# Dense attention's score matmuls: 289 contraction rows cut into two passes of 128 and a shared pass of 33, instead of 97, 96 and 96

## The chip, the cores and the metric

The kernel runs on one core of one Trainium2 chip. The metric is device time in microseconds of one execution. Of the core's engines, TensorE (PE) multiplies, with a separate path for its weight loads (PEld), VectorE is DVE, ScalarE is ACT, GpSimd is POOL, and SyncE (SP) issues most DMAs.

## The reference

One layer of a transformer over 1024 latent tokens and 256 context tokens. The part that the change touches is group B of its attention, eight heads of latent attention, dense over all 1280 keys:

```python
def mla_attend(qn, qr, kn, kr, v):
    s = (jnp.einsum('bqhd,bkhd->bhqk', qn, kn, preferred_element_type=jnp.float32)
         + jnp.einsum('bqhr,bkr->bhqk', qr, kr, preferred_element_type=jnp.float32)) * MLA_SCALE
    p = jax.nn.softmax(s, axis=-1)
    o = jnp.einsum('bhqk,bkhd->bqhd', p.astype(v.dtype), v)
    return o.reshape(qn.shape[0], qn.shape[1], H_B * V_B)
```

`qn` and `kn` have 64 values per head, `qr` and `kr` have 32 (`kr` is shared by the heads). Before it stand the input projection and a windowed attention (group A), after it the output projection, a router, and 16 experts.

## The kernel before, in words

All matmuls that matter are in fp32r. Where one factor alone isn't exact enough, a value is split into a high part and the remainder (`split`), and a product is taken as high x high + high x low + low x high. For a score that is 3 x 96 rows of contraction, and one row more that adds the negative maximum of the query's scores, so that the exponential needs no bias: 289 rows. The kernel before holds them in four tiles per head: `kh` (97 rows: 64 of `kn`, 32 of `kr`, one of ones) and `kl` (96 rows, the low parts) for the keys, `qh` (97 rows, the last one the negative maximum) and `ql` for the queries.

Dense attention (group B) is a loop over 160 units, 8 heads x 2 halves of the queries x 10 blocks of 128 keys (`Runner.run`, which emits the program in order). A unit's scores are a tile of 128 keys by 512 queries in a PSUM bank "s", from three matmuls (`s_b`, L1093 to L1095). ACT takes the exponential twice, into `ph` (rounded, L614) and again in full (L615), in place for the even units and into the buffer `pf` for the odd ones. The difference, `pl`, is made by DVE for even units and by POOL for odd ones (L1098). Four units later, three matmuls add the unit to the head's output in a bank "x" (`pv_b`, L1107 to L1109).

Between the units stand the steps that prepare the next head (`prep_b`, spread over the 20 units of the head before): `kprep` splits its keys (L954 to L960), `tr` transposes its queries (L976) and splits them (L978, L979), `mxp` and `mxq` multiply queries and keys once more for the maxima (L983, L990, in banks "m", reduced by DVE at L985 and L992), and `fin2` sends the negative maxima as a row to `qh` (L1005, a DMA that POOL issues). Head 0 is prepared before the loop, mixed with the rest of the key and value projection (`kn_mm`, L875, evacuated by ACT at L877). `kr_copy` (L932) copies the rows of `kr`, which are the same for all heads, to the second pair of key tiles.

Other work hangs in the same loop: `mod_rest` streams 8 MB of modulation weights through the staging tiles (`stage`), and `load_wo` loads the output projection's weights, 1 MB a call, into them. After the loop `omm` (L1138) multiplies the first 128 tokens of the mixed heads with these weights, split by `wo_split` one after the other. The last 128 rows of the mix, from the last two heads, come back from memory at L1205 (`mix7`).

Elsewhere in the program, matmuls use few rows of the array at L564 (one row, `finish_fast`) and L1540 (two rows, `pick2` of the experts). The built program gives every matmul the part of the array, the tile, that it uses: these two have 32 of its 128 rows, L1108 has all rows and 64 columns, the router's L1353 and the matmuls named above have the whole array.

Of the kernel before, what the change touches and what calls it, by code (L numbers as in the profile page):

```python
# [10 lines left out]
F32 = mybir.dt.float32  # L11
F32R = mybir.dt.float32r
# [5 lines left out]
PSUM = bass.MemoryType.PSUM  # L18
DRAM = bass.MemoryType.DRAM

D = 1024
S = 1024
# [3 lines left out]
NK = NT + NCT  # L26
# [12 lines left out]
def f32(ap):  # L39
    return ap.bitcast(F32)  # L40
# [7 lines left out]
def tile_backbone(ctx: ExitStack, tc, x, c, ctxt, c_ctx, w_mod, b_mod, norm_attn, norm_ffn, w_in,  # L48
# [104 lines left out]

    psa = Pool("psa", space=PSUM)

    def bank(tag, shape=(128, 512)):
        return psa.tile(list(shape), F32, tag, bufs={"s": 3, "x": 2, "m": 3}[tag])

    qaf = qa.rearrange("p t e -> p (t e)")
    brow, mr = qaf[0:1, 0:2 * D], qaf[0:4, 2 * D:4 * D]  # L160
# [764 lines left out]
    kn, vb = B2["kn"], B2["vb"]  # L925

    pbk2 = Pool("pbk2")
    khs = [pbk2.tile([97, NK * 128], F32R, f"kh{i}") for i in range(2)]
    kls = [pbk2.tile([96, NK * 128], F32R, f"kl{i}") for i in range(2)]
    pbq = Pool("pbq")  # L930

    def kr_copy():  # L932
        act.copy(khs[1][64:96, :], f32(khs[0][64:96, :]))
        act.copy(kls[1][64:96, :], f32(kls[0][64:96, :]))

    for (t0, t1), pt in zip(TG, krt):
        sl = slice(t0 * 128, t1 * 128)
        split(act, dve, khs[0][64:96, sl], kls[0][64:96, sl], pt[:32, :(t1 - t0) * 128])
    for q in range(2):
        dve.tensor_copy(khs[q][96:97, :], ones[0:1, 0:1].to_broadcast([1, NK * 128]))  # L940
# [4 lines left out]

    def prep_b(h):
        st = {}
        kh, kl, vv = khs[h % 2], kls[h % 2], vh[h % 2]
        steps = []

        def kprep():
            src = kn[:, h // 2]
            if h % 2 == 0:
                act.activation(kh[0:64, :], src[0:64], AF.Copy)  # L954
                pool.tensor_sub(kl[0:64, :], src[0:64], f32(kh[0:64, :]))
            else:
                scr = pbq.tile([128, NK * 128], F32R, "scr")
                act.activation(kh[0:64, :], src[64:128], AF.Copy)
                dve.tensor_copy(scr[64:128], src[64:128])
                pool.tensor_sub(kl[0:64, :], src[64:128], f32(scr[64:128]))  # L960

        def vprep():
            src = vb[:, :, h * 64:(h + 1) * 64]
            dve.tensor_copy(vv[:, :, 0:64], src)
            pool.tensor_sub(vv[:, :, 66:130], src, f32(vv[:, :, 0:64]))

        def alloc():
            st["q"] = pbq.tile([97, S], F32R, "qh", bufs=2)
            st["l"] = pbq.tile([96, S], F32R, "ql", bufs=2)
            QB[h] = (st["q"], st["l"], kh, kl, vv)  # L970
            st["m"] = pbq.tile([128, 8, 3], F32, "mx", bufs=2)

        def tr(b):
            pt = bank("m")
            for j in range(4):
                pe.transpose(pt[:96, j * 128:(j + 1) * 128], qb[:, 4 * b + j, h * 96:(h + 1) * 96], ident)  # L976
            sl = slice(b * 512, (b + 1) * 512)
            act.activation(st["q"][0:96, sl], pt[:96], AF.Copy)  # L978
            dve.tensor_sub(st["l"][:, sl], pt[:96], f32(st["q"][0:96, sl]))  # L979

        def mxp(t, j):
            pm = bank("m")
            pe.matmul(pm, st["q"][0:96, t * 128:(t + 1) * 128], kh[0:96, j * 512:(j + 1) * 512],  # L983
                      start=True, stop=True)
            dve.tensor_reduce(out=st["m"][:, t, j:j + 1], in_=pm, axis=AX.X, op=OP.max)  # L985

        def mxq(t):
            pm = bank("m").rearrange("p (a b) -> p a b", a=2)
            for j in range(2):
                pe.matmul(pm[:, j], st["q"][0:96, (t + j) * 128:(t + j + 1) * 128], kh[0:96, 1024:1280],  # L990
                          start=True, stop=True)
            dve.tensor_reduce(out=st["m"][:, t:t + 2, 2], in_=pm, axis=AX.X, op=OP.max)  # L992

        def fin():
            nm = pbq.tile([128, 8], F32, "nm", bufs=2)
            dve.tensor_reduce(out=nm, in_=st["m"], axis=AX.X, op=OP.max, negate=True)
            st["nm"] = nm

        def fin2():
            nm = st["nm"]  # L1000
            pt = bank("m")
            pe.transpose(pt[:8, :128], nm, ident)
            rr = pbq.tile([8, 128], F32R, "rr", bufs=2)
# [42 lines left out]

    wof = {}
    NX = 6
    slots = [0, 1, 2, 3]

    def stage():
        n = slots.pop(0)
        slots.append(n)
        return (wms if n < 4 else wms2 if n < 6 else wms3 if n < 6 + NX else pm).tile([128, 2, D], F32, f"wst{n}")

    def load_wo(k):
        w = stage()
# [26 lines left out]
    R.add(150, lambda: early_mix(0, 3))  # L1084
    R.add(151, lambda: early_mix(3, 7))

    def s_b(u, un):
        h, hf, kc, first, last = un
        qh, ql, kh, kl, vv = QB[h]
        ps = bank("s")  # L1090
        ks = slice(kc * 128, (kc + 1) * 128)
        qs = slice(hf * 512, (hf + 1) * 512)
        pe.matmul(ps, kh[:, ks], qh[:, qs], start=True, stop=False)  # L1093
        pe.matmul(ps, kh[0:96, ks], ql[:, qs], start=False, stop=False)  # L1094
        pe.matmul(ps, kl[:, ks], qh[0:96, qs], start=False, stop=True)  # L1095
        on_dve = not (u % 2 and u < len(units) - 8)
        pf, ph, lo = softmax_parts(pbt, ps, SC_B, on_dve)
        return ph, lo, lambda: (dve if on_dve else pool).tensor_sub(lo, pf, f32(ph))  # L1098

    def pv_b(u, un, pp):  # L1100
        h, hf, kc, first, last = un
        ph, lo, _ = pp
        vv = QB[h][4]
        if first:
            xo[h, hf] = bank("x", (65, 512))
        xx = xo[h, hf]
# [14 lines left out]
                    R.add(R.u + d, f)  # L1121

    late_b = R.run(units, s_b, pv_b, 4)
    psa.close()
# [689 lines left out]
```

## Time and profile before

| what | us |
|---|---|
| median of 3 runs | 1218.68 (1218.54 to 1219.02) |
| the profiled execution's time | 1217.52 |
| its span, first to last instruction | 1215.8 |
| dense attention's units in the span | 440.3 to 719.8 |

Busy time over the whole span: PE 92%, PEld 69%, DVE 73%, ACT 58%, POOL 38%. TensorE's granted clock is 0.959 of full speed on average. These shares are means over stages with different limits, so the stage that is changed has to be read by itself. In rows of the trace the first number is the start in microseconds from the span's start, the second the duration; a matmul's record is longer than the time that it keeps the array from the next one.

### The profile page before, as it was taken

To read this page: it belongs to the slowest core of one execution; us is meant where nothing else is said; L and a number is where in the kernel's file an instruction comes from. 1 tells how busy PE (TensorE), PEld (TensorE's weight loads), DVE (VectorE), ACT (ScalarE), POOL (GpSimd) and SP (SyncE) were. 2 spreads that over 40 slices of the span, in tenths; PEclk is the share of its full clock that TensorE was granted. 3 is DMA by queue.
4 is the path that set the end of the run, shared out by engine and by line. 5 is a ranking of instruction groups with operands and counts; after the bars stand their busy time and mean duration, and the time that the engine had idled before them with its cause. 6 is when DMAs were issued, how large, how long until landed. Compare 5 with 4: busy or idle time off the path is not lost. (4 is left out here: it accounts for less than half of the span.)

```text
span 1215.8 us, 15361 instructions
## 1 busy us (share of the span) xinstructions
PE 1115.5 (92%) x5168; PEld 838.1 (69%) x5168; DVE 884.1 (73%) x1511; ACT 700.6 (58%) x1122; POOL 463.7 (38%) x453
## 2 busy tenths in 40 slices
PE   7799998899999889999999999996499999999993
PEld 1687886576667567776666577885377887778872
DVE  5767764656874466777777256588789999999986
ACT  5623223567776447776676772223176776777753
POOL 0042322455443244665655432442314243332214
PEclk9899999999999889999999999997599999999996
DMA  7714320001211110212010525755799999999727
GB/s 297 298 59 131 129 76 1 1 15 23 66 28 23 22 73 32 88 53 87 17 45 10 187 74 200 243 194 206 277 319 371 375 371 386 370 397 372 279 51 278
DMA packets 68622, 198.27 MB, mean 163 GB/s; under 512 B 15894, under 2 KB 24243, under 8 KB 63423
## 3 DMA queue, kind: packets, MB, share of 16 engines
q1 hardware_dynamic: 60224, 178.73, 40.5%
q0 software_dynamic: 5152, 18.52, 5.7%
q8 instruction: 40, 0.66, 0.2%
q10 hardware_dynamic: 3168, 0.06, 0.1%
q14 instruction: 38, 0.31, 0.1%
HBM read 172.34 MB, written 24.78 MB: 162 GB/s over the span
## 5 line engine op out<-in xcount | busy, mean ns | idle before, releaser
L1409 DVE TENSOR_TENSOR wl<-wst,wh 128x2048 fp32r<-128x2048 f32 x95 | 215.9, 2287 | 22.3 <-ACT wh L1403 22.3
L1403 ACT ACTIVATE wh<-wst 128x2048 fp32r<-128x2048 f32 x96 | 183.8, 1917 | 71.8 <-PE u L1580 39.3
L614 ACT ACTIVATE ph<-s 128x512 fp32r<-128x512 f32 x236 | 140.8, 597 | 92.5 <-PE s L1095 75.9
L1098 POOL TENSOR_TENSOR pl<-pf,ph 128x512 fp32r<-128x512 f32 x76 | 102.2, 1355 | 68.2 <-ACT pf L615 46.1
L1098 DVE TENSOR_TENSOR pl<-s,ph 128x512 fp32r<-128x512 f32 x84 | 57.0, 680 | 54.6 <-ACT s L615 54.6
L985 DVE TENSOR_REDUCE mx<-m 128x1 f32<-128x512 f32 x128 | 83.1, 682 | 14.3 <-PE m L983 14.1
L615 ACT ACTIVATE s<-s 128x512 f32<-128x512 f32 x123 | 73.1, 594 | 0.0
L1093 PE MATMUL s<-qh,kh 97*128 97x512 f32 x160 | 66.1, 413 | 5.2 <-DVE pl L1098 2.7
L1626 PE MATMUL y<-wh,shf 128*128 128x512 f32 x240 | 69.4, 400 | 0.0
L615 ACT ACTIVATE pf<-s 128x512 f32<-128x512 f32 x113 | 66.9, 592 | 0.0
L772 POOL TENSOR_TENSOR pl<-pf,ph 128x512 fp32r<-128x512 f32 x37 | 47.7, 1289 | 49.2 <-ACT pf L615 45.9
L122 POOL TENSOR_SCALAR rstd<-ss 128x1 f32<-128x1 f32 x36 | 12.9, 358 | 134.6 <-ACT sjunk L193 64.6
L1094 PE MATMUL s<-ql,kh 96*128 96x512 f32 x160 | 64.1, 401 | 0.0
L1107 PE MATMUL x<-ph,vh 128*65 128x512 f32 x160 | 63.8, 399 | 0.0
L1095 PE MATMUL s<-qh,kl 96*128 96x512 f32 x160 | 63.6, 397 | 0.0
L1108 PE MATMUL x<-ph,vh 128*64 128x512 f32 x160 | 63.3, 396 | 0.0
L1109 PE MATMUL x<-pl,vh 128*65 128x512 f32 x160 | 63.2, 395 | 0.0
L329 PE MATMUL s<-wih,hb 128*128 128x512 f32 (+2 forms) x224 | 57.7, 381 | 3.3 <-ACT hb L81 3.3
L1548 POOL DMA_INDIRECT xg<-h2d,ix x16 | 23.6, 1473 | 91.4 <-PE t L1564 36.4
L1643 POOL DMA_INDIRECT accd<-yt,ix x7 | 34.7, 4959 | 61.2 <-DVE yt L1636 61.2
L81 ACT ACTIVATE hb<-xt 128x512 fp32r<-128x512 f32 (+1 forms) x22 | 13.0, 593 | 69.2 <-DVE xt L245 69.1
L1643 POOL DMA_INDIRECT accd<-gab,ix x8 | 25.3, 3164 | 70.1 <-DVE gab L1636 70.1
(491 smaller groups left out, 3135.9 us busy)
## 6 DMA issues: line engine op xcount, KB each, us to landing
wst<-in_w_gate_dram SPq DMA_DIRECT2D x63, 512.0 KB
wst<-in_w_up_dram SPq DMA_DIRECT2D x63, 512.0 KB
wst<-in_w_down_dram SPq DMA_DIRECT2D x31, 1024.0 KB
mw<-in_w_mod_dram SPq DMA_DIRECT2D x32, 256.0 KB
wst<-in_w_mod_dram SPq DMA_DIRECT2D x8, 1024.0 KB
wi<-in_w_in_dram SPq DMA_DIRECT2D x8, 720.0 KB
wi<-in_w_mod_dram SPq DMA_DIRECT2D x9, 512.0 KB
h2d<-h SPq DMA_DIRECT2D x8, 520.0 KB
```

Source lines behind the costliest of these rows:

```text
L614: act.activation(ph, ps, AF.Exp, scale=scale)
L615: act.activation(pf, ps, AF.Exp, scale=scale)
L985: dve.tensor_reduce(out=st["m"][:, t, j:j + 1], in_=pm, axis=AX.X, op=OP.max)
L1093: pe.matmul(ps, kh[:, ks], qh[:, qs], start=True, stop=False)
L1094: pe.matmul(ps, kh[0:96, ks], ql[:, qs], start=False, stop=False)
L1095: pe.matmul(ps, kl[:, ks], qh[0:96, qs], start=False, stop=True)
L1098: return ph, lo, lambda: (dve if on_dve else pool).tensor_sub(lo, pf, f32(ph))
L1107: pe.matmul(xx, vv[:, kc, 0:65], ph, start=first, stop=False)
L1108: pe.matmul(xx[0:64], vv[:, kc, 66:130], ph, start=False, stop=False)
L1403: act.activation(W[i][0], staged[i], AF.Copy)
L1409: eng.tensor_sub(lo, staged.pop(i), f32(hi))
L1626: pe.matmul(py[n], a[:, k], w[b][:, n], start=(k == 0 and m == 0), stop=(k == 3 and m == 2))
```

## The change

The 289 rows are laid out anew. A first pass of 128 rows has `kn` and `kr` high with `qn` and `qr` high, and 32 rows of `kn` low with `qn` high. A second has `kn` and `kr` high with `qn` and `qr` low, and the other 32 rows of `kn` low with `qn` high. The rest is 33 rows: `kr` low with `qr` high, and the row of ones with the negative maximum. That rest is held twice, in `k3` and `q3` on partitions 0 to 32 and 64 to 96. For every two units (two blocks of keys) two matmuls of 33 rows are issued first, one from each half of the partitions, into two banks; then each unit follows with its two passes of 128 rows. The rows that stand in more than one place are copied there by DMAs from SP (`kr_copy`, `kprep`, `tr`); `kr_copy` no longer uses ACT. The row of the negative maximum is sent twice by POOL.

The banks go from 3 "s", 2 "x", 3 "m" to 4, 2 and 2, the `pf` buffers from three to two, and one of four staging tiles goes: the load of the last two blocks of output weights (`load_wo(6)`) moves from the loop to a place after it.

```diff
+    PSP = [psa, {"s": 3, "x": 2, "m": 3}]
...
+    k1s = [pbk2.tile([128, NK * 128], F32R, f"kh{i}") for i in range(2)]
+    k2s = [pbk2.tile([128, NK * 128], F32R, f"kl{i}") for i in range(2)]
+    k3 = pbk2.tile([97, NK * 128], F32R, "k3")
...
-    def kr_copy():
-        act.copy(khs[1][64:96, :], f32(khs[0][64:96, :]))
-        act.copy(kls[1][64:96, :], f32(kls[0][64:96, :]))
...
+        split(act, dve, k1s[0][64:96, sl], k3[0:32, sl], pt[:32, :(t1 - t0) * 128])
+
+    def kr_copy():
+        for o in (k1s[1], k2s[0], k2s[1]):
+            nc.sync.dma_start(out=f32(o[64:96, :]), in_=f32(k1s[0][64:96, :]))
+        nc.sync.dma_start(out=f32(k3[64:96, :]), in_=f32(k3[0:32, :]))
...
+            nc.sync.dma_start(out=f32(k2[0:64, :]), in_=f32(kh[0:64, :]))
+            nc.sync.dma_start(out=f32(kh[96:128, :]), in_=f32(sc[0:32]))
+            nc.sync.dma_start(out=f32(k2[96:128, :]), in_=f32(sc[32:64]))
...
+            for o, r in ((st["q"][96:128], 0), (st["l"][96:128], 32), (st["3"][0:32], 64), (st["3"][64:96], 64)):
+                nc.sync.dma_start(out=f32(o[:, sl]), in_=f32(st["q"][r:r + 32, sl]))
...
-            pool.dma_start(out=st["q"][96:97, :], in_=rr)
+            for o in (32, 96):
+                pool.dma_start(out=st["3"][o:o + 1, :], in_=rr)
...
-    PB[:] = [3, 5]
+    PB[:] = [2, 5]
...
-    slots = [0, 1, 2, 3]
+    slots = [0, 1, 2]
...
-    for k in range(0, 8, 2):
+    for k in range(0, 6, 2):
         R.add(132 + 2 * k, lambda k=k: load_wo(k))
...
+    psa.close()
+    psb = Pool("psb", space=PSUM)
+    PSP[:] = [psb, {"s": 4, "x": 2, "m": 2}]
+    SB = {}
...
-        pe.matmul(ps, kh[:, ks], qh[:, qs], start=True, stop=False)
-        pe.matmul(ps, kh[0:96, ks], ql[:, qs], start=False, stop=False)
-        pe.matmul(ps, kl[:, ks], qh[0:96, qs], start=False, stop=True)
+        if kc % 2 == 0:
+            SB[u], SB[u + 1] = bank("s"), bank("s")
+            for j in range(2):
+                o = 64 * j
+                pe.matmul(SB[u + j], k3[o:o + 33, (kc + j) * 128:(kc + j + 1) * 128], q3[o:o + 33, qs],
+                          start=True, stop=False)
+        ps = SB.pop(u)
+        pe.matmul(ps, kh[:, ks], q1[:, qs], start=False, stop=False)
+        pe.matmul(ps, k2[:, ks], q2[:, qs], start=False, stop=True)
...
-    slots[:0] = [4, 5]
+    slots[:0] = [3, 4, 5]
+    load_wo(6)
```

In PE's order, a unit of the loop before, with the maxima of the next head ahead of it ("s" are the scores, "x" the head's output, "m" the maxima):

```order
L983 MATMUL m<-kh_4283,qh 128x512
L990 MATMUL m<-kh_4283,qh 128x256 x2
L1093 MATMUL s<-qh,kh_4284 128x512
L1094 MATMUL s<-ql,kh_4284 128x512
L1095 MATMUL s<-qh,kl_4286 128x512
L1107 MATMUL x<-ph,vh_4299 65x512
L1108 MATMUL x<-ph,vh_4299 64x512
L1109 MATMUL x<-pl,vh_4299 65x512
```

The same place of the changed program, an even unit and the start of the odd one behind it:

```order
L995 MATMUL m<-kh_4283,qh 128x512
L1002 MATMUL m<-kh_4283,qh 128x256 x2
L1114 MATMUL s<-q_5987,k_4287 128x512 x2
L1117 MATMUL s<-qh,kh_4284 128x512
L1118 MATMUL s<-ql,kl_4286 128x512
L1130 MATMUL x<-ph,vh_4300 65x512
L1131 MATMUL x<-ph,vh_4300 64x512
L1132 MATMUL x<-pl,vh_4300 65x512
L995 MATMUL m<-kh_4283,qh 128x512 x2
L1117 MATMUL s<-qh,kh_4284 128x512
```

The two L1114 are the pair of 33 rows, for this unit and the next. Every unit has two score matmuls of its own. The built program gives the first of a pair rows 0 to 63 of the array and the second rows 64 to 127.

In SP's order after the loop, in the changed program (`mixd` is the mixed heads in memory, `xres` the residual, the `qb` row is the last part of the mix):

```order
L1139 DMA mixd_61<-ou 64x512
L1139 DMA mixd_62<-ou 64x512
L1071 DMA wst_7455<-in_w_out_dram 128x2x1024
L1208 DMA xres<-in_x_dram 128x1024 x2
L1248 DMA h_7506<-in_norm_ffn_dram 128x1024
L1250 DMA wrf<-in_w_router_dram 128x8x16
L1229 DMA qb<-mixd_61 128x256
```

The row of L1071 is new here; before, it stood in the loop.

## Rows read from the trace of the kernel before

**Rows 1.** Busy time by stretch: length, busy of each engine, clock, DMA share, GB/s.

```profile
440.00:720.00 280.00, 275.62 (x1216) 193.31 (x1217) 188.40 (x283) 198.57 (x370) 159.25 (x123) 0.99 0.21 69
```

**Rows 2.** Groups by line: forms, count, busy us, mean ns, idle before.

```profile
L1093 PE MATMUL s<-qh,kh 97*128 97x512 f32 x160 | 66.1, 413 | 5.2 <-DVE pl L1098 2.7 <-DMA qh<-rr 2.6
L1098 POOL TENSOR_TENSOR pl<-pf,ph 128x512 fp32r<-128x512 f32 x76 | 102.2, 1355 | 68.2 <-ACT pf L615 46.1 <-PE m L990 7.0 <-PE m L983 6.2
L985 DVE TENSOR_REDUCE mx<-m 128x1 f32<-128x512 f32 x112 | 73.0, 682 | 9.7 <-PE m L983 9.6
```

**Rows 3.** Timeline of PE in the loop: start, duration, rows*columns of the weights.

```profile
564.02 0.40 PE L1094 MATMUL s<-ql,kh 96*128 96x512 f32 x1
564.25 0.39 PE L1095 MATMUL s<-qh,kl 96*128 96x512 f32 x1
564.48 0.39 PE L1107 MATMUL x<-ph,vh 128*65 128x512 f32 x1
564.71 0.40 PE L1108 MATMUL x<-ph,vh 128*64 128x512 f32 x1
564.95 0.40 PE L1109 MATMUL x<-pl,vh 128*65 128x512 f32 x1
```

**Rows 4.** Timeline of the weight loads, the same place.

```profile
564.71 0.14 PEld L1109 LDWEIGHTS x<-pl,vh 128*65 128x65 f32 x1
```

**Rows 5.** Timeline of PE around two-row matmuls of the experts.

```profile
887.39 0.40 PE L1580 MATMUL u<-wh,xl 128*128 128x512 f32 x1
887.72 0.60 PE L1540 MATMUL t<-ones,scf 2*128 2x1 f32 x4
888.25 0.50 PE L1580 MATMUL a<-wh,xh 128*128 128x512 f32 x1
888.59 0.39 PE L1580 MATMUL u<-wh,xh 128*128 128x512 f32 x1
```

**Rows 6.** Timeline of the weight loads there; idle time in brackets.

```profile
887.16 0.19 PEld L1580 LDWEIGHTS u<-wh,xl 128*128 128x128 f32 x1
887.72 0.52 PEld L1540 LDWEIGHTS t<-ones,scf 2*128 2x128 f32 x4 [0.37 <-issue]
888.25 0.19 PEld L1580 LDWEIGHTS a<-wh,xh 128*128 128x128 f32 x1
```

**Rows 7.** L1540 as a whole: min/median/max ns; idle time before it, times.

```profile
L1540 PE MATMUL t<-ones,scf x28: 245/245/267, 887.7 to 1092.4; 2*128 2x1 f32 x28
  issue: 2.6, 7
```

**Rows 8.** Timelines of PE and of its loads around the router's L1353.

```profile
752.60 0.62 PE L1138 MATMUL o<-woh,qb 128*128 128x512 f32 x2
752.82 1.09 PEld L1353 LDWEIGHTS r<-wrf,th 128*128 128x128 f32 x8
```

**Rows 9.** Timeline of ACT before the loop.

```profile
411.33 1.25 ACT L933 CAST kh<-kh 32x1280 fp32r<-32x1280 f32 x1
```

**Rows 10.** Timeline of PE there, and the stretch that follows by engine.

```profile
415.34 0.80 PE L875 MATMUL m<-cvh,wkh 128*128 128x512 f32 x1 [3.49 <-ACT kn L877]
415.00:420.00 5.00, 4.66 (x16) 3.95 (x17) 0.90 (x2) 2.44 (x6) 2.91 (x1) 0.50 0.00 0
```

**Rows 11.** Timeline of POOL at the loop's start, and a wait of PE (total, times, longest).

```profile
438.37 0.81 POOL L1005 DMA_DIRECT2D qh<-rr  x1 [20.36 <-ACT rr L1004]
PE s L1093 <- DMA qh<-rr: 2.6, 1, 2.6
```

**Rows 12.** After the loop: timelines of SP, ACT and PE, and one stretch.

```profile
725.37 0.82 SPq L1184 DMA_DIRECT2D xres<-in_x_dram  x2
734.14 0.31 ACT L81 ACTIVATE qb<-qb 128x128 fp32r<-128x128 f32 x1 [6.92 <-DMA qb<-mixd]
734.50 1.09 PE L1138 MATMUL o<-woh,qb 128*128 128x512 f32 x2 [2.19 <-ACT qb L81]
728.00:731.00 3.00, 3.00 (x15) 2.48 (x14) 3.00 (x3) 0.00 (x0) 0.00 (x0) 1.00 1.01 353
```

More of the change, by code (lines that the diff above doesn't have):

```diff
@@ L154, in tile_backbone @@
     psa = Pool("psa", space=PSUM)
+    PSP = [psa, {"s": 3, "x": 2, "m": 3}]
     def bank(tag, shape=(128, 512)):
-        return psa.tile(list(shape), F32, tag, bufs={"s": 3, "x": 2, "m": 3}[tag])
+        return PSP[0].tile(list(shape), F32, tag, bufs=PSP[1][tag])
     qaf = qa.rearrange("p t e -> p (t e)")
@@ L927, in tile_backbone @@
     pbk2 = Pool("pbk2")
-    khs = [pbk2.tile([97, NK * 128], F32R, f"kh{i}") for i in range(2)]
-    kls = [pbk2.tile([96, NK * 128], F32R, f"kl{i}") for i in range(2)]
+    k1s = [pbk2.tile([128, NK * 128], F32R, f"kh{i}") for i in range(2)]
+    k2s = [pbk2.tile([128, NK * 128], F32R, f"kl{i}") for i in range(2)]
+    k3 = pbk2.tile([97, NK * 128], F32R, "k3")
     pbq = Pool("pbq")
-    def kr_copy():
-        act.copy(khs[1][64:96, :], f32(khs[0][64:96, :]))
-        act.copy(kls[1][64:96, :], f32(kls[0][64:96, :]))
     for (t0, t1), pt in zip(TG, krt):
         sl = slice(t0 * 128, t1 * 128)
-        split(act, dve, khs[0][64:96, sl], kls[0][64:96, sl], pt[:32, :(t1 - t0) * 128])
-    for q in range(2):
-        dve.tensor_copy(khs[q][96:97, :], ones[0:1, 0:1].to_broadcast([1, NK * 128]))
+        split(act, dve, k1s[0][64:96, sl], k3[0:32, sl], pt[:32, :(t1 - t0) * 128])
[4 more added lines that the diff above has]
+    for o in (32, 96):
+        dve.tensor_copy(k3[o:o + 1, :], ones[0:1, 0:1].to_broadcast([1, NK * 128]))
     vh = [pbq.tile([128, NK, 130], F32R, f"vh{i}") for i in range(2)]
@@ L947, in prep_b @@
         st = {}
-        kh, kl, vv = khs[h % 2], kls[h % 2], vh[h % 2]
+        kh, k2, vv = k1s[h % 2], k2s[h % 2], vh[h % 2]
         steps = []
@@ L952, in kprep @@
             src = kn[:, h // 2]
+            sc = pbq.tile([128, NK * 128], F32R, "scr")
             if h % 2 == 0:
                 act.activation(kh[0:64, :], src[0:64], AF.Copy)
-                pool.tensor_sub(kl[0:64, :], src[0:64], f32(kh[0:64, :]))
+                pool.tensor_sub(sc[0:64], src[0:64], f32(kh[0:64, :]))
             else:
-                scr = pbq.tile([128, NK * 128], F32R, "scr")
                 act.activation(kh[0:64, :], src[64:128], AF.Copy)
-                dve.tensor_copy(scr[64:128], src[64:128])
-                pool.tensor_sub(kl[0:64, :], src[64:128], f32(scr[64:128]))
+                dve.tensor_copy(sc[64:128], src[64:128])
+                pool.tensor_sub(sc[0:64], src[64:128], f32(sc[64:128]))
+            nc.sync.dma_start(out=f32(k2[0:64, :]), in_=f32(kh[0:64, :]))
+            nc.sync.dma_start(out=f32(kh[96:128, :]), in_=f32(sc[0:32]))
+            nc.sync.dma_start(out=f32(k2[96:128, :]), in_=f32(sc[32:64]))
         def vprep():
@@ L967, in alloc @@
         def alloc():
-            st["q"] = pbq.tile([97, S], F32R, "qh", bufs=2)
-            st["l"] = pbq.tile([96, S], F32R, "ql", bufs=2)
-            QB[h] = (st["q"], st["l"], kh, kl, vv)
+            pl_ = pbt if h % 2 else pbq
+            st["q"] = pl_.tile([128, S], F32R, "qh")
+            st["l"] = pl_.tile([128, S], F32R, "ql")
+            st["3"] = pl_.tile([97, S], F32R, "q3")
+            QB[h] = (st["q"], st["l"], st["3"], kh, k2, vv)
             st["m"] = pbq.tile([128, 8, 3], F32, "mx", bufs=2)
@@ L978, in tr @@
             act.activation(st["q"][0:96, sl], pt[:96], AF.Copy)
-            dve.tensor_sub(st["l"][:, sl], pt[:96], f32(st["q"][0:96, sl]))
+            dve.tensor_sub(st["l"][0:96, sl], pt[:96], f32(st["q"][0:96, sl]))
+            for o, r in ((st["q"][96:128], 0), (st["l"][96:128], 32), (st["3"][0:32], 64), (st["3"][64:96], 64)):
+                nc.sync.dma_start(out=f32(o[:, sl]), in_=f32(st["q"][r:r + 32, sl]))
         def mxp(t, j):
@@ L1004, in fin2 @@
             act.activation(rr, pt[:8, :128], AF.Copy)
-            pool.dma_start(out=st["q"][96:97, :], in_=rr)
+            for o in (32, 96):
+                pool.dma_start(out=st["3"][o:o + 1, :], in_=rr)
         steps += [kprep, alloc, lambda: tr(0), lambda: tr(1)] + ([lambda: None] if h else [])
@@ L1053, in stage @@
         slots.append(n)
-        return (wms if n < 4 else wms2 if n < 6 else wms3 if n < 6 + NX else pm).tile([128, 2, D], F32, f"wst{n}")
+        return (wms if n < 3 else wms2 if n < 6 else wms3 if n < 6 + NX else pm).tile([128, 2, D], F32, f"wst{n}")
     def load_wo(k):
@@ L1085, in tile_backbone @@
     R.add(151, lambda: early_mix(3, 7))
+    psa.close()
+    psb = Pool("psb", space=PSUM)
+    PSP[:] = [psb, {"s": 4, "x": 2, "m": 2}]
+    SB = {}
     def s_b(u, un):
         h, hf, kc, first, last = un
-        qh, ql, kh, kl, vv = QB[h]
-        ps = bank("s")
+        q1, q2, q3, kh, k2, vv = QB[h]
         ks = slice(kc * 128, (kc + 1) * 128)
         qs = slice(hf * 512, (hf + 1) * 512)
-        pe.matmul(ps, kh[:, ks], qh[:, qs], start=True, stop=False)
-        pe.matmul(ps, kh[0:96, ks], ql[:, qs], start=False, stop=False)
-        pe.matmul(ps, kl[:, ks], qh[0:96, qs], start=False, stop=True)
+        if kc % 2 == 0:
[7 more added lines that the diff above has]
+        pe.matmul(ps, k2[:, ks], q2[:, qs], start=False, stop=True)
         on_dve = not (u % 2 and u < len(units) - 8)
@@ L1102, in pv_b @@
         ph, lo, _ = pp
-        vv = QB[h][4]
+        vv = QB[h][5]
         if first:
@@ L1123, in tile_backbone @@
     late_b = R.run(units, s_b, pv_b, 4)
-    psa.close()
+    psb.close()
     pso = Pool("pso", space=PSUM)
```

## The prediction, made before the changed kernel ran

> **What bounds the kernel now.** I read four views in turn: the busy times by stretch, the groups of instructions by line, the timeline of TensorE with that of its weight loads, and the waits. Dense attention's unit loop runs from 440.3 to 719.8 us of the span. In that stretch PE is busy for 275.6 of 280 us, while DVE has 188, ACT 199 and POOL 159 [rows 1]: PE alone bounds the loop. A unit issues three score matmuls (160 of each, [rows 2]) and three for the values. Their records overlap, so the mean of 0.40 us is no price; the price is the distance from start to start. In the timeline four such steps take 564.95 - 564.02 = 0.93 us, so one matmul of 512 columns costs a slot of **0.233 us** whatever its rows and columns [rows 3]. It can be that short because each weight load is issued as the matmul before it starts: the load for L1109 begins at 564.71, with L1108 [rows 4].
>
> **The change part by part.**
>
> *Two slots become a pair.* Of every two units' twelve slots the change keeps ten and replaces the two others by two 33-row matmuls, one on rows 0 to 63 of the array, one on rows 64 to 127. There are 160 / 2 = 80 such pairs. If the two ran together and nothing else changed, a pair would cost one slot, and the change would give 80 x 0.233 = 18.6 us.
>
> The question is what it costs to go from whole-array matmuls to half-array ones and back, 80 times. The loop before never does it, so I bound it by the nearest rows that use part of the array's rows: L1540 (2 rows), which the built program puts on a tile of 32 rows. The matmul before it starts at 887.39, but the next load is not issued with it; it comes at 887.72, 0.33 us later, close to the end of that matmul's record, after 0.37 us in which the load path waited for nothing that the profile shows [rows 5, 6]. That idle time stands before all seven bursts of L1540, 2.6 us in all [rows 7]. On the way back the load and its matmul are recorded together at 888.25, and the next one follows at 888.59, 0.34 us later instead of 0.233: the load itself, 0.107 us, is exposed [rows 5, 6]. So crossing costs 0.33 + 0.107 = 0.44 us from one matmul's start to the next one's, against 0.233. It isn't the plain fp32 of these matmuls: L1353 is plain fp32 on the whole array, and its load is issued at 752.82, with the second L1138 matmul (752.60 + 0.23) [rows 8].
>
> With that price, from the last whole matmul to the first of the pair is 0.44, between the two of the pair one exposed load, 0.11 (four L1540 matmuls take 0.60 us, one lasts 0.245, so their pitch is 0.12; [rows 5, 7]), and out again 0.44: 0.99 us, where three slots took 0.70. That is +0.29 a pair, 80 x 0.29 = **+23.2 us**. If the second load costs nothing, it is 0.88 - 0.70 = +0.18, or +14.4 us; if the second matmul waits for the first (0.233), +0.41, or +33 us. I take +23.2, the value of the row in which loads follow each other within a tile.
>
> One row of the loop itself speaks the other way: L1108 writes 64 columns, the built program gives it a tile of 64 columns, and it still keeps the 0.233 us slot on both sides [rows 3]. In the Trainium skill, "TensorEngine Tiling (Array Packing)", section Key Properties, says that any change of tiling mode drains TensorE; by it L1108 would pay too, which the trace denies, so the rule isn't general. By the rule the pair pays, as in my sum; by L1108's row it would not, which is the first rival.
>
> *First head.* `kr_copy` leaves ACT: two copies of 1.25 us, of which one stands in [rows 9], that stand between PE and a free "m" bank, while PE idles 3.49 us and comes back at half clock, 0.50 in the five microseconds after [rows 10]. Without them the idle time is some 1.0 us: 2.5 us gained. In the half-clocked stretch PE is busy 4.66 of 5 us, at full clock half of that, so up to 2.3 us more. Bounds 0 (if something else then holds PE) to -4.8, taken **-4.0**: the 2.5, and most of the clock. The row of the maxima is now sent twice by POOL, each issue 0.81 us, and PE already waits 2.6 us for the one [rows 11]: **+0.8** once; later heads have several units between issue and use.
>
> *The other copies.* SP gets 3 + 8 more DMAs a head. At 0.41 us an issue (two in 0.82, [rows 12]) that is 4.5 us of the 35 us that a head takes, and what they carry is used a head later; the cover is the 15 or so units between `tr` and the next head. So nothing, and a copy would have to be some 20 us late to cost anything.
>
> *Banks and buffers.* Scores go from three banks to four, allocated by two. At an even unit PE then asks for what it asked before, the bank of three units back, and one older. Maxima go from three banks to two: a slot of at most two maxima is followed by 1.4 us of scores and values, in which DVE can empty both (0.68 us each, [rows 2]). The buffers of the second exponential go from three to two: POOL needs 1.36 us of the 3.5 us of two units [rows 2]. With a slower PE all three get more room, so nothing; where PE gets faster, up to +3.
>
> *After the loop.* `load_wo(6)`, 1 MB, moves from the middle of the loop to SP's place before the loads of the residual. Behind it in that queue stands the last row of the mix, which lands in time for ACT at 734.14 while PE waits for it, 2.19 us [rows 12]. The queues move 353 GB/s there [rows 12], so 1 MB ahead is 1.05 / 0.353 = 3.0 us more, and PE has nothing else to do: **+3.0** (0 if room in the queues ahead of it takes it, as a bound that no row excludes; 5 if the longer pause halves PE's clock for some 4 us behind it, as at 415 [rows 10]).
>
> Sum: 23.2 - 4.0 + 0.8 + 3.0 = **+23.0 us**. The profiled execution took 1217.52 us (span 1215.8); the median of the runs is 1218.68, 1.2 more, and I add to the median: **1242 us**.
>
> **The rivals.**
>
> *No crossing cost, the pair overlaps (faster).* If tiles of this kernel's fp32r operands are entered like L1108's, loads stay ahead of their matmuls, and the second of the pair starts one load, 0.11 us, after the first: a pair saves 0.233 - 0.11 = 0.12, 9.8 us in all. With the other terms (-0.2) that is 1208 to 1209. It decides as soon as a crossing costs less than half a saved slot, 0.06 us. For it: L1108, and that the rows which pay are all plain fp32. Against it: L1108 cuts columns, not rows, and every row-cut burst in the trace pays. In the Trainium skill, "TensorE: Matmul & The Clock Gate", section Measured speedup vs the span model, tiles that share the array start about 4 ns apart. By that figure the saving would be estimated at 18 us, the time at 1200; no row here shows two row tiles in flight.
>
> *Crossing paid, no overlap (much slower).* The second matmul waits for the first: +33 us, with its load exposed as well +41. 1252 to 1259. The trace has no case of two tiles at once, so only the lack of evidence speaks for it.
>
> *The change does nothing.* No crossing, no overlap: two slots remain two slots, and the small terms cancel (-0.2): 1218.5. For it: a slot costs 0.233 whatever its rows are [rows 3].
>
> **How the numbers follow.** The forecast's own case has 0.56: its range runs from 14.4 - 4.8 + 0.8 + 0 = +10 (1229) to 24 + 0.8 + 5 + 2 = +32 (1250). Paid without overlap 0.12, no crossing with overlap 0.22, nothing 0.10. A measurement of this kernel tells 0.2%, 2.4 us, from no change. Faster by more: 0.22 and a little of the last case, 0.25. Within: 0.06. Slower: 0.69, from the first two and the remainder. As two signs hold much of the chance, the range of 8 in 10 reaches from 1206, into the faster rival, to 1251; that of the likeliest case alone is 1229 to 1250.
>
> **What would show it.** In the timeline of the changed kernel, look at the 160 rows of L1114 and their weight loads. Right: the first load of a pair comes some 0.33 us after the matmul before it, PE's load path shows "issue" idle time there, and L1117 after a pair begins with its load; two units take 11 slots plus about 0.5 us. Wrong: L1114 rows 0.23 us or less apart with loads ahead of them, and a loop shorter than 280 us. The head's pause at 411 to 415 should shrink, and the one before the last mix row should grow by 3 us. If PE waits in the loop for DVE at L995 or for the exponentials at L1114, the buffers weren't free of cost.

## The result, and the profile after

The changed kernel takes **1238.56 us** (median of 4 runs, 1236.62 to 1239.57) against 1218.85 us of the kernel before on the same chip: a ratio of 1.0168, 95% interval 1.0139 to 1.0197, so 17 to 24 us slower. The forecast was 1242, its range 1206 to 1251, with a chance of 0.69 for slower. Its sign and size hold; of its terms, the runs below show, three were not what it said, and a fourth is not settled.

The profiled execution took 1237.99 us (span 1236.0, granted clock 0.954; before 1217.52, 1215.8 and 0.959). Dense attention's loop, [rows 1], from the first score's start to the last value matmul's:

| part of the span, us | before | after | difference |
|---|---|---|---|
| up to the first score | 440.31 | 442.15 | +1.84 |
| the unit loop | 279.26 | 293.98 | +14.72 |
| the output projection (to the last L1138, now L1161) | 112.64 | 117.28 | +4.64 |
| the rest | 383.60 | 382.56 | -1.04 |

The busy times by stretch of the loop: length, busy time of PE, weight loads, DVE, ACT and POOL, clock, DMA share, GB/s.

```profile
442.00:450.00 8.00, 7.85 (x24) 4.86 (x24) 3.58 (x6) 4.44 (x9) 5.46 (x4) 0.67 0.50 109
450.00:736.00 286.00, 281.61 (x1191) 167.08 (x1191) 179.94 (x278) 194.83 (x361) 157.76 (x121) 1.00 0.32 90
```

PE is still the bound, 281.6 of 286 us, and at full clock. The rest of the page's shape is as before: DVE, ACT and POOL do the same work in a longer loop. The groups by line that answer to [rows 2]:

```profile
L1114 PE MATMUL s<-q,k 33*128 33x512 f32 x160 | 40.9, 500 | 2.6 <-ACT kh L963 2.6
L1117 PEld LDWEIGHTS s<-qh,kh 128*128 128x128 f32 x160 | 30.2, 189 | 24.7 <-issue 19.8
L997 DVE TENSOR_REDUCE mx<-m 128x1 f32<-128x512 f32 x112 | 73.6, 683 | 21.7 <-PE m L995 21.2
```

160 records of L1114 with a mean of 0.50 us make 40.9 us busy, not 80: two lie upon each other. The timeline of PE at one even unit, against [rows 3]:

```profile
565.25 0.40 PE L1132 MATMUL x<-pl,vh 128*65 128x512 f32 x1
565.49 0.67 PE L995 MATMUL m<-kh,qh 96*128 96x512 f32 x2
566.09 0.51 PE L1114 MATMUL s<-q,k 33*128 33x512 f32 x2
566.52 0.50 PE L1117 MATMUL s<-qh,kh 128*128 128x512 f32 x1
566.86 0.39 PE L1118 MATMUL s<-ql,kl 128*128 128x512 f32 x1
567.09 0.40 PE L1130 MATMUL x<-ph,vh 128*65 128x512 f32 x1
567.32 0.40 PE L1131 MATMUL x<-ph,vh 128*64 128x512 f32 x1
567.55 0.40 PE L1132 MATMUL x<-pl,vh 128*65 128x512 f32 x1
```

And its weight loads, against [rows 4, 6]:

```profile
565.26 0.19 PEld L995 LDWEIGHTS m<-kh,qh 96*128 96x128 f32 x1
566.09 0.19 PEld L1114 LDWEIGHTS s<-q,k 33*128 33x128 f32 x2 [0.25 <-ACT pf L617]
566.52 0.19 PEld L1117 LDWEIGHTS s<-qh,kh 128*128 128x128 f32 x1 [0.25 <-issue]
566.63 0.19 PEld L1118 LDWEIGHTS s<-ql,kl 128*128 128x128 f32 x1
```

What to see: the load of the pair is not issued with the matmul before it, but starts together with the pair, at 566.09; both loads and both matmuls of the pair are one record of 0.19 and 0.51 us. L1117's load too starts with its matmul (566.52), 0.43 us after the pair's, and only L1118's comes ahead of its matmul again (566.63, the matmul at 566.86). All 80 pairs have it so: the load of the pair's first matmul and that of the L1117 behind the pair start at most 0.03 us before their matmuls, where the load of L1131 starts 0.227 us (median) before its own. The group of L1114 over the whole loop (min/median/max ns, then what the load path waited for):

```profile
L1114 PEld LDWEIGHTS s<-q,k x160: 182/183/285, 442.1 to 730.7; 33*128 33x128 f32 x160
L1114 PE MATMUL s<-q,k x160: 490/498/789, 442.1 to 730.7; 33*128 33x512 f32 x160
  issue: 15.4, 43
```

Over all 80 pairs the medians of the distances from start to start are: into the pair 0.33 us (0.32 in the 33 pairs behind L1132, where the kernel before has 0.23 from L1109 to L1093; 0.21 in the 13 behind the 256 columns of L1002, where it has 0.12), between its two matmuls 0.003, to L1117 0.43, from there to L1118 0.34. From the matmul ahead of the pair to L1118 the median is 1.094 us; the same stretch before, with the slot of the other unit, is four steps of 0.231 to 0.236, 0.937. The pair costs **+0.157 us, 12.6 us in 80 pairs**.

The first head, against [rows 10]: PE's timeline, and the stretches that follow by engine.

```profile
416.53 0.50 PE L877 MATMUL m<-cvh,wkh 128*128 128x512 f32 x1 [1.06 <-ACT kn L879]
421.12 0.39 PE L877 MATMUL m<-cvh,wkh 128*128 128x256 f32 x1 [2.50 <-DVE ql L989]
420.00:425.00 5.00, 3.44 (x13) 2.16 (x13) 4.21 (x10) 0.38 (x1) 0.00 (x0) 0.84 0.65 150
425.00:440.00 15.00, 13.55 (x37) 8.44 (x36) 10.67 (x19) 1.96 (x5) 0.00 (x0) 0.71 0.05 13
```

The pause of 3.49 us for ACT has shrunk to 1.06, but 4.6 us later there is one of 2.50, for DVE's subtraction: 3.56 us in all, and a clock of 0.84 and 0.71 behind it. The first pair of the loop stands apart: the row of maxima is sent to it twice, and its second load waits for the second sending (PE's loads):

```profile
442.65 0.28 PEld L1114 LDWEIGHTS s<-q,k 33*128 33x128 f32 x1 [0.25 <-DMA q<-rr]
```

The first load of that pair is at 442.12, so the second sending costs this one pair 0.5 us. After the loop, against [rows 12], the timelines of SP, ACT and PE:

```profile
741.93 0.39 SPq L1071 DMA_DIRECT2D wst<-in_w_out_dram  x1
744.71 3.77 SPq L1229 DMA_DIRECT2D qb<-mixd  x1
754.24 0.31 ACT L81 ACTIVATE qb<-qb 128x128 fp32r<-128x128 f32 x1 [4.43 <-DMA qb<-mixd]
748.91 0.73 PE L1161 MATMUL o<-woh,qb 128*128 128x512 f32 x2 [1.39 <-ACT woh L81]
754.60 1.22 PE L1161 MATMUL o<-woh,qb 128*128 128x512 f32 x2 [3.14 <-ACT qb L81]
751.00:756.00 5.00, 1.86 (x5) 1.17 (x4) 1.67 (x4) 1.35 (x3) 0.00 (x0) 0.51 1.07 323
```

PE waits 3.14 us for the last row of the mix where it waited 2.19, and 1.39 for the split of the output weights that now come late. In the five microseconds around the pause the granted clock is 0.51, about the lower of the two levels (1.2 of 2.4 GHz).

### The profile page after: what moved, and what is told of

The parts are those of the page before. It is cut to its first block, busy times and chain, and to the rows that moved or that the text cites. A ratio compares the mean times of both kernels' runs of the same rounds, so it can differ in the third digit from the quotient of the medians.

```text
span 1236.0 us, 15500 instructions
## 1 busy us (share of the span) xinstructions
PE 1132.2 (92%) x5168; PEld 818.5 (66%) x5168; DVE 879.8 (71%) x1511; ACT 699.5 (57%) x1120; POOL 470.1 (38%) x461
## 5 line engine op out<-in xcount | busy, mean ns | idle before, releaser
L1121 POOL TENSOR_TENSOR pl<-pf,ph 128x512 fp32r<-128x512 f32 x76 | 103.3, 1369 | 75.1 <-ACT pf L617 33.3
L1121 DVE TENSOR_TENSOR pl<-s,ph 128x512 fp32r<-128x512 f32 x84 | 57.2, 681 | 63.0 <-ACT s L617 31.5
L1117 PE MATMUL s<-qh,kh 128*128 128x512 f32 x160 | 73.5, 460 | 0.0
L1118 PE MATMUL s<-ql,kl 128*128 128x512 f32 x160 | 63.4, 396 | 0.0
L1132 PE MATMUL x<-pl,vh 128*65 128x512 f32 x160 | 63.0, 394 | 0.0
L1131 PE MATMUL x<-ph,vh 128*64 128x512 f32 x160 | 62.9, 393 | 0.0
L1130 PE MATMUL x<-ph,vh 128*65 128x512 f32 x160 | 62.8, 393 | 0.0
L995 PE MATMUL m<-kh,qh 96*128 96x512 f32 x128 | 50.0, 438 | 3.9 <-DVE ql L989 1.4
```

Of the source, the lines that this page charges most:

```text
L1117: pe.matmul(ps, kh[:, ks], q1[:, qs], start=False, stop=False)
L1118: pe.matmul(ps, k2[:, ks], q2[:, qs], start=False, stop=True)
L1130: pe.matmul(xx, vv[:, kc, 0:65], ph, start=first, stop=False)
L1131: pe.matmul(xx[0:64], vv[:, kc, 66:130], ph, start=False, stop=False)
L1132: pe.matmul(xx, vv[:, kc, 0:65], lo, start=False, stop=last)
```

## The experiments

The theory: the loop's loss is the way into the half-array pair and out of it, and that is more than the slot that the pair saves. Its first rivals: the pair does not overlap at all; every small matmul costs, not the change of mode; the loss is in banks, buffers and copies. Ratios are to the kernel before, timed on the same chip in the same session; 0.1% is 1.2 us.

**The rest as one whole-array matmul** (`e1_rest_whole`). Rows 33 to 64 of the keys are zero.

```diff
-                pe.matmul(SB[u + j], k3[o:o + 33, (kc + j) * 128:(kc + j + 1) * 128], q3[o:o + 33, qs],
+                pe.matmul(SB[u + j], k3[0:65, (kc + j) * 128:(kc + j + 1) * 128], q3[0:65, qs],
```

> The changed kernel with the rest of 33 rows as one whole-array matmul of 65 rows a unit: rows 33 to 64 of its keys are zeros, so the scores are the same. All else of the change stays: four banks for scores, two for maxima, pairs of units, the copies by SP's DMAs, the later load of the output weights. Theory A, the crossing between whole-array and half-array matmuls costs 0.163 us a pair beyond the saved slot: no crossing and nothing beside anything, so six slots a unit again, the loop from the first score to the end of the last values falls from 294.0 to 279-282 us, and the time to 1223-1226. Rival B, the loop's loss comes from the banks, buffers or copies: these are all still there, the loop stays at 290 or more and the time at 1235-1240. In both the 4.6 us after the loop and the 1.8 us gained at the first head stay.

Measured: 1225.45 us, ratio 1.0027 (1.0011 to 1.0044). PE's timeline has no gap around the same two matmuls, which are now two slots, and their loads go ahead of them:

```profile
564.95 0.42 PE L1002 MATMUL m<-kh,qh 96*128 96x256 f32 x2
565.21 0.64 PE L1112 MATMUL s<-q,k 65*128 65x512 f32 x2
565.68 0.40 PE L1115 MATMUL s<-qh,kh 128*128 128x512 f32 x1
```

From L1112 to L1115 it is 565.68 - 565.21 = 0.47, two plain slots. So it is the half-array form that costs, as theory A has it; the same data on the whole array are entered and left at 0.23. But the loop took 285.5 us, above the 279 to 282 that I expected: 6.3 more than before, with six slots a unit as before, and so only 8.5 below the changed kernel's. Waits of PE in that loop (total, times, longest):

```profile
PE m L995 <- DVE mx L997: 2.0, 3, 1.1
PE m L995 <- DVE ql L989: 1.9, 5, 0.4
PE s L1112 <- DVE pl L1119: 1.4, 1, 1.4
```

PE waits for DVE to give back banks of maxima. That is a second cost that the theory did not hold; `e8_before_banks` below takes it up.

**Both of the pair on the same half** (`e2_same_half`).

```diff
-                o = 64 * j
+                o = 0
```

> The changed kernel with both 33-row matmuls of a pair on the same half of the array's rows, 0 to 63; the scores are the same. Theory A, the two of a pair really run beside each other now, since they start 3 ns apart: on one half the second waits for the first, 0.233 us later, 80 times, +18.6 us, 1255-1259. Rival B, that the pair is fast because small tiles pipeline anyway or that the two halves share one stream: the pair's pitch and the time stay, 1237-1240. Between the two: the second load is exposed only, 0.11 us a pair, +9 us, 1247.

Measured: 1251.02 us, ratio 1.0235 (1.0216 to 1.0254), 0.7% above the changed kernel's 1.0168. The time lies below theory A's 1255 to 1259, nearer to the 1247 of the value between, so the totals alone would not decide; the distance does: over 80 pairs the median from the first L1114 to the second is 0.3375 us instead of 0.003, and from the second to L1117 0.323. The whole stretch is 0.23 us longer. In the timeline:

```profile
566.51 0.40 PE L995 MATMUL m<-kh,qh 96*128 96x512 f32 x1
566.84 0.73 PE L1114 MATMUL s<-q,k 33*128 33x512 f32 x2
567.51 0.50 PE L1117 MATMUL s<-qh,kh 128*128 128x512 f32 x1
```

So the two do run beside each other in the changed kernel, and take turns when they stand on one half: the saving of one slot is real. The loop grew by 13.7 us and not by 80 x 0.23 = 18.4, since a slower PE waits less for DVE (its waits for maxima and for the subtraction fall from 3.6 us in the changed kernel to 1.5).

**The pair twice** (`e3_pair_twice`).

```diff
+            for j in (0, 1):
+                o = 64 * j
+                pe.matmul(SB[u + j], k3[o:o + 33, (kc + j) * 128:(kc + j + 1) * 128], q3[o:o + 33, qs],
+                          start=True, stop=True)
```

> The changed kernel with every pair issued twice, the second writing the same banks over the first; the scores are the same. Theory A, what costs is the change of mode, once into the half-array pair and once out: the second pair follows in the same mode and costs one slot, 0.233 us, +18.6 us for 80 pairs, 1255-1259. Rival B, every half-array matmul holds its load back until the one before it on any rows has ended: the second pair costs as much as a crossing, 0.33 + 0.10 us, +34 us, 1270-1275. If two pairs on the same rows and into the same banks need more than either, the start-to-start distance of the two pairs shows it.

Measured: 1249.97 us, ratio 1.0229 (1.0208 to 1.0250). The timelines of PE and of the loads:

```profile
564.50 0.50 PE L1114 MATMUL s<-q,k 33*128 33x512 f32 x2
564.84 0.40 PE L1118 MATMUL s<-q,k 33*128 33x512 f32 x2
565.17 0.50 PE L1121 MATMUL s<-qh,kh 128*128 128x512 f32 x1
564.50 0.19 PEld L1114 LDWEIGHTS s<-q,k 33*128 33x128 f32 x2
564.61 0.19 PEld L1118 LDWEIGHTS s<-q,k 33*128 33x128 f32 x2
565.17 0.19 PEld L1121 LDWEIGHTS s<-qh,kh 128*128 128x128 f32 x1 [0.37 <-issue]
```

Behind the first pair the second one's loads come at once (564.61, 0.11 after), as loads do in the whole-array stream, and are not held back to its end; only L1121's load, the first one back on the whole array, is. The second pair starts 0.34 us after the first: the 0.11 of the first pair's load, which the way in exposes, and a slot of 0.23. The whole stretch with two pairs is 0.23 us longer than with one, by the medians, one slot; rival B wanted 0.43. So theory A: the price is per change of mode, in and out, and a second pair in the same mode would cost one slot in place of two. The time misses theory A's range of 1255 to 1259: the loop took 308.7 us and grew by 14.7, not by 80 x 0.23 = 18.4. As in the run before, PE waits less for DVE (1.3 us in the loop instead of 3.6); the rest of the difference is not put down to a row.

**The last row of the mix first** (`e4_mix_row_first`).

```diff
     load_wo(6)
+    src7 = mixd[0].rearrange("(k p) t -> p k t", p=128)[:, 7:8, 0:256]
+    nc.sync.dma_start(out=EQ["m"][:, 7:8], in_=src7)
...
-    mix7()
```

> The changed kernel with the load of the last row of the mix put ahead of the loads of the residual in SP's queue, behind the last load of the output weights alone. Theory A, the time lost after the loop is queueing: 1 MB moved behind the loop delays the row that PE waits for. Then PE's pause of 3.14 us before that row shrinks to 0-1 us, and the time falls by 2-4 us, 1234-1236. Rival B, the row itself is late (its data aren't written before) or the residual takes its place as the thing waited for: 1237-1239.

Measured: 1234.84 us, ratio 1.0105 (1.0088 to 1.0122) against 1.0168. PE's long pause is gone, those for the weights are not (PE's timeline):

```profile
753.01 0.73 PE L1161 MATMUL o<-woh,qb 128*128 128x512 f32 x2 [1.24 <-ACT woh L81]
754.27 1.18 PE L1161 MATMUL o<-wol,qb 128*128 128x512 f32 x2 [0.53 <-DVE wol L89]
759.95 0.74 PE L1161 MATMUL o<-qb,mixl 128*128 128x512 f32 x2 [0.62 <-DVE mixl L89]
```

The output projection takes 113.4 us instead of 117.3. So that pause is a matter of the queue, theory A. By the ratios the gain is 0.63%, some 8 us, more than these 3.9; the two intervals allow from 2 to 13. The loop, whose code is that of the changed kernel, took 297.0 us in this profile, 3.0 more than in the profile of the change, with a clock of 0.55 in the seven microseconds from 443 and 0.93 in the fifty from 450.

**The banks alone** (`e8_before_banks`, from the kernel before).

```diff
+    psa.close()
+    psb = Pool("psb", space=PSUM)
+    PSP[:] = [psb, {"s": 4, "x": 2, "m": 2}]
```

> The kernel before with one part of the change alone: in the unit loop four PSUM banks for scores and two for maxima instead of three and three. Theory A, that the third bank for maxima is what the loop of the run with the whole-array rest lacks (its loop took 285.5 us, 6.3 us more than before, and its matmuls L995 and L1002 wait for DVE's maxima): the loop goes from 279.3 to 283-287 us, PE waits at L983 and L990 for DVE's maxima several times, and the time rises by 4-7 us, 1223-1228. Rival B, the prediction's own step: a slot of at most two maxima leaves DVE time to empty both, so nothing changes, 1218-1221; then the 6.3 us come from the copies or the buffers of the second exponential.

Measured: 1225.39 us, ratio 1.0053 (1.0032 to 1.0074); the loop takes 284.5 us. Waits of PE in the loop; the kernel before has 1.3 us of waits for maxima there, and none for `ql`:

```profile
PE m L985 <- DVE mx L987: 2.3, 3, 1.2
PE m L985 <- DVE ql L981: 1.8, 5, 0.4
```

The longest of them, in the timelines of DVE and PE:

```profile
557.62 2.16 DVE L817 SCALAR_TENSOR_TENSOR gfb<-wst,cs,gfb 128x1024 f32<-128x1024 f32 x1
561.03 1.10 PE L985 MATMUL m<-kh,qh 96*128 96x512 f32 x2 [1.19 <-DVE mx L987]
```

DVE is at the modulation weights (`mod_rest`) for 2.16 us and at a unit's `pl` behind that, before it comes to the maxima. Theory A: with this edit alone the loop is 5.2 us longer, so two banks for maxima are not enough at the pace of the kernel before. All waits for maxima and `ql` in the loop are 5.2 us, 3.9 more than before, and the one for `pl` is 1.5 shorter, so the waits account for 2.4 of the loop's 5.2 us; the rest is not put down to a row.

**Three banks each in the changed kernel** (`e9_after_banks3`).

```diff
-    PSP[:] = [psb, {"s": 4, "x": 2, "m": 2}]
+    PSP[:] = [psb, {"s": 3, "x": 2, "m": 3}]
```

> The changed kernel with three banks for scores and three for maxima in the loop, as before the change; a pair still takes two banks for scores at once. Theory A, two banks for maxima cost 4-6 us of the loop: the waits for DVE's maxima go, the loop falls from 294 to 288-290 us, the time by 4-6 us, to 1233-1236. Rival B, three banks for scores are too few where two are asked for at once: PE waits at L1114 for exponentials about 0.1-0.3 us a pair, which gives back 8-24 us, and the time is the same or longer, 1238-1255.

Measured: 1246.04 us, ratio 1.0225 (1.0199 to 1.0251), longer than the changed kernel: rival B. The waits for maxima are gone (0.2 us left), but the second of a pair has to wait for its bank. The group of L1114's loads over the whole loop, and PE's timeline at one pair:

```profile
L1114 PEld LDWEIGHTS s<-q,k 33*128 33x128 f32 x160 | 25.3, 184 | 41.4 <-issue 21.5 <-ACT pf L617 9.8 <-ACT kh L963 2.8
564.63 0.82 PE L1114 MATMUL s<-q,k 33*128 33x512 f32 x2
565.38 0.50 PE L1117 MATMUL s<-qh,kh 128*128 128x512 f32 x1
```

The median distance between the two of a pair is 0.148 us instead of 0.003, the loop 303.5 us. So in this loop the pair needs four banks for scores, and with two for the head's output two are left for the maxima. One bank for the output and three for maxima was not tried.

**Neither pairs nor banks** (`e11_whole_banks3`, the whole-array rest again, unit by unit).

```diff
-    PSP[:] = [psb, {"s": 4, "x": 2, "m": 2}]
+    PSP[:] = [psb, {"s": 3, "x": 2, "m": 3}]
...
-        ps = SB.pop(u)
+        ps = bank("s")
+        pe.matmul(ps, k3[0:65, ks], q3[0:65, qs], start=True, stop=False)
```

> The changed kernel with both parts of the loop's cost taken back and the rest kept: the rest of 33 rows is one whole-array matmul of 65 rows in each unit, no pairs, three banks for scores and three for maxima. What is left of the change is the copies by DMA, two buffers of the second exponential instead of three, and the later load of the output weights. Theory A, pairs and banks are all of the loop's loss: the loop takes 279-281 us, as before, and the time is 1219-1223, 0-3 us over before (the load after the loop). Rival B, buffers or copies cost something too: the loop takes 283 us or more, 1224 or more.

Measured: 1219.08 us, ratio 0.9991 (0.9978 to 1.0003), and the loop 279.39 us where before has 279.26. Copies by DMA, two buffers of the second exponential instead of three and the later load of the weights together cost nothing that can be measured: theory A. That is their sum: in this profile the output projection took 117.7 us (112.6 before), and the way from the first transposes of the keys' rest to the first score 36.0 (38.8 before), so a loss by the load and a gain at the first head may stand against each other.

**`kr_copy` alone off ACT** (`e5_before_kr_dma`, from the kernel before).

```diff
-        act.copy(khs[1][64:96, :], f32(khs[0][64:96, :]))
-        act.copy(kls[1][64:96, :], f32(kls[0][64:96, :]))
+        nc.sync.dma_start(out=f32(khs[1][64:96, :]), in_=f32(khs[0][64:96, :]))
+        nc.sync.dma_start(out=f32(kls[1][64:96, :]), in_=f32(kls[0][64:96, :]))
```

> The kernel before with the two copies of kr_copy sent by SP's DMAs instead of two instructions of ACT; nothing else. Theory A, the prediction's step: these copies are the pause of 3.49 us at 415, and without them PE waits 1.0 us there and gets its clock back sooner: 2.5-4 us less, 1215-1218 where before has 1219-1221. Rival B, as in the profile of the change, DVE's subtraction behind the next transposes is late next (2.5 us at 421): the gain is 0-1.8 us.

Measured: 1219.89 us, ratio 1.0001 (0.9985 to 1.0018). The pauses of PE:

```profile
416.86 0.50 PE L875 MATMUL m<-cvh,wkh 128*128 128x512 f32 x1 [1.07 <-ACT kn L877]
421.36 0.39 PE L875 MATMUL m<-cvh,wkh 128*128 128x256 f32 x1 [2.40 <-DVE ql L979]
```

1.07 + 2.40 = 3.47 us, as much as the 3.49 before [rows 10]. Rival B, at its end of no gain: DVE was as late as ACT. The interval still allows a gain of 1.8 us.

**The best version found** (`e10_before_mix_row`, the kernel before with the mix row's edit alone, and `e6_before_both`, with that and `kr_copy` by DMA).

> The kernel before with only the last row of the mix loaded ahead of the residual after the loop; kr_copy stays on ACT. Theory A, the gain of the run with both edits (0.5%) is all of this one: the pause before that row goes, and with it the five microseconds at half clock behind it, 4-6 us in all, 1213-1216 where before has 1219-1220. Rival B, the two edits only gain together, since kr_copy's DMAs took 0 alone and the row's pause is 2.2-3.2 us: 2-3 us, 1216-1218.

> The kernel before with kr_copy's copies by SP's DMAs and the last row of the mix loaded ahead of the residual after the loop. Theory A, both pauses are PE's alone and add: 2-4 us at the first head and 2 us after the loop (the pause of 2.19 us goes), 4-6 us in all, 1214-1217, faster than both kernels. Rival B, each pause is taken over by what is late next: under 2 us, no difference that can be measured.

Measured: 1216.54 us, ratio 0.9970 (0.9952 to 0.9987) for the row alone, and 1214.16 us, ratio 0.9951 (0.9934 to 0.9967) for both: **faster than both kernels**. In the second, PE has no pause before the row and no low clock behind it, where the kernel before had 0.97 and 0.69 (five-microsecond stretches):

```profile
730.00:735.00 5.00, 5.00 (x24) 4.03 (x22) 4.02 (x7) 0.00 (x0) 0.00 (x0) 1.00 0.86 274
735.00:740.00 5.00, 5.00 (x23) 4.13 (x22) 2.93 (x5) 2.49 (x6) 0.96 (x3) 1.00 0.92 361
```

The output projection takes 109.7 us there and 110.4 with the row alone, against 112.6 before and 117.6 in `e5_before_kr_dma`, whose code there is that of before. The row alone gains 3.7 us (1.6 to 5.9), between its two theories; both edits gain 6.0 (4.0 to 8.0), theory A. So most of the gain is the row's. Whether `kr_copy` adds to it stays open: the two intervals overlap, and alone it gave nothing that can be measured.

## Why the prediction was right, and where its terms were not

*Two slots become a pair: right in kind, too large.* The forecast took 0.44 us in, 0.11 for the second load, 0.44 out. The way in and out is what it said: counted like there, to the end of the exposed load, the medians give 0.32 + 0.11 = 0.43 in, and 0.43 from the pair to L1117 with its load at the start. The "issue" idle time and L1117's load with its matmul are there as foretold. The term that was mis-sized is the **second load, taken from the row of four matmuls on one tile**: 0.003 us, since the loads of two tiles run together. The sum by that is the forecast's other value, +14.4; measured +12.6. So two units take 11 slots and 0.39 us, where 11 slots and about 0.5 were to be the sign of it. The rule that it weighed stands in the Trainium skill, "TensorEngine Tiling (Array Packing)", section Key Properties: a change of tiling mode drains TensorE. The trace agrees for tiles that cut the rows, 80 times in and 80 times out. It does not for L1131, L1108 before, which cuts columns: from L1130 at 567.09 to L1131 at 567.32 and on to L1132 at 567.55 are plain slots. The Trainium skill, "TensorE: Matmul & The Clock Gate", section Measured speedup vs the span model, has some 4 ns between tiles. The 3 ns here agree. The first rival had the overlap right, with 0.11 us between the two, and fell by its other half, that entering would be free.

*Banks and buffers: wrong.* The step said that a slot of two maxima leaves DVE time to empty both banks. It failed: alone, the banks make the kernel before 0.53% slower, 3.9 to 9.0 us, and a whole-array rest with them 1.0027 against 0.9991 without. What it overlooked is that DVE does not come to the maxima at once: the waits are for `ql` and for maxima that stand behind other work of DVE, such as the 2.16 us of `mod_rest` above. (The two runs with the whole-array rest differ also in the order of issue, by two units or by one.) In the changed kernel less of it is left: PE waits 3.6 us for maxima and `ql`, 2.3 more than before. In exchange the wait of 2.7 us for DVE's `pl` [rows 2] is gone, presumably since PE comes there later; no run tests that alone.

So the loop's +14.7: pairs 12.6, maxima 2.3, less 2.7, 0.5 for the second sending of the row to the first pair, and an estimated 1 us from a lower clock in its first eight microseconds (0.67, before 0.79, (0.79 - 0.67) x 8). That makes 13.7; 1 us is not put down to a row, and the same loop took 3 us more in the profile of `e4_mix_row_first`.

*First head: wrong in its pause, open in its size.* -4.0 was taken, 2.5 of it for a pause that shrinks to 1.0 us. That step failed: `ql` on DVE holds PE as long as ACT did, 3.56 us in all, and the bound named for it, "0 (if something else then holds PE)", is what the pause came to. The 1.84 us that stand before the first score in the table are no effect of the change: over the twelve profiles of this study the transposes of the keys' rest ahead of it, up to which the order of the work is the same in all, start anywhere from 400.86 to 408.18 us (401.49 before, 405.14 in the changed kernel). From those transposes to the first score the changed kernel took 37.0 us and the kernel before 38.8. PE's idle time in that stretch is the same, 7.6 and 7.8; the difference lies in its busy time, 29.4 and 31.0, at a clock of 0.84 and 0.82. In the three profiles with `kr_copy` on ACT the stretch took 36.9 to 39.3 us, at clocks from 0.91 to 0.80, in the nine with DMAs 33.6 to 37.2, at 0.97 to 0.83. So up to 1.8 us may be gained through the clock; the runs' times neither show nor exclude it. The +0.8 for the second sending of the row was near: PE waits 2.60 us for the first, as it did for the one before, and 0.5 for the second.

*The other copies: right.* `e11_whole_banks3` keeps nearly all of them and its loop is as long as before's, at 95 GB/s instead of 69 in the queues.

*After the loop: right in kind, its size not settled.* The pause grew by 0.95 us and another 1.92 came (the weights' split on ACT and DVE), 2.9 in all, as the 3.0 of the forecast. But the sign that was named, 3 us more in the one pause before the row, did not come, and the wait for the weights themselves had no term. And profiles of kernels with before's code in this place took 112.6, 114.9 and 117.6 us, as they got 2.2 to 3.3 us of pause and more or less of the low clock behind it; the six with the late load and the old place of the row took 114.6 to 119.6. `e11_whole_banks3`, one of these, is as fast as before in all. So 4.6 is one pair of executions, and the effect of the load alone is somewhere from 0 to 5.

The sum came out near since the terms' errors cancel, and that is luck: the pair 23.2 for 12.6, the first head -4.0 for 0 to -1.8, the banks 0 for some 2 in the changed loop. With the terms as measured the sum is 12.6 + 2.3 - 2.7 + 0.5 + 3 = 15.7 us, or 14 with the first head's 1.8, and 17 to 24 were measured; at least 1 us, and up to 10, is open. In the two profiles 3.7 of the 20.2 us of difference stand ahead of those transposes, where the work is the same.

## What to carry to other kernels

Two matmuls on separate halves of the array's rows do run together, but each group of them within a stream of whole-array matmuls pays for the way in and the way out, 0.157 + 0.233 = 0.39 us here, against 0.233 for each slot saved. So count the pairs of a group and the banks that they need before packing: one pair a group loses, and two, an estimate from the run with the pair twice, would win 0.08 us a group (0.39 against two slots of 0.233), but want banks that this loop has not (that was not tried). Where PE waits for two engines one behind the other, taking work from the first may only move the wait, as from 3.49 us to 1.06 and 2.50 here; where it waits for a small load, look at what was queued ahead of it for no reason.

## What was not expected of the hardware

- Loads of two row halves are recorded 3 ns apart, and so are their matmuls (medians of 80 pairs), where loads within one tile follow each other at 0.11 us. And within the mode a next load goes ahead of its matmul as usual (0.11 us after the first pair's start, in the run with the pair twice); only the first load after a change of mode waits, 0.32 us from the start of the matmul before it into the pair and again out of the second pair.
- A pause of 3.14 us of PE came with a granted clock of 0.51 in its five microseconds, the lower of the two levels, after PE had been busy for 9.72 of the ten microseconds from 736 on and for 3.09 of the next five, both at 1.00. Without these pauses, in `e6_before_both`, the clock was 1.00 in both stretches shown.
- Profiles of the same work differ by 7 us in the start of one stage (400.86 to 408.18), by 5 in the length of another (112.6 to 117.6) and by 3 in the changed kernel's loop (294.0 and 297.0). One profile against one other proves no term under some 5 us; a distance from start to start, taken 80 times, does.
